# The row maxima of causal attention: mask addition and maximum in one VectorE instruction per score block

## The chip, the cores and the metric

The kernel runs on one core of one Trainium2 chip. The metric is the device time of one launch in microseconds (us); lower is better. The kernel before takes 1011.64 us, the median of three runs (1011.25 to 1013.38). The engines are named as in the profile: PE is TensorE's matrix multiplication and PEld its weight load, DVE is VectorE, ACT is ScalarE, POOL is GpSimd, SP is SyncE, whose queue (SPq) issues most transfers.

## The reference, cut to what matters

One layer of a decoder with four token mixers in parallel, on 1024 tokens (and 16 learned tokens ahead of them) of 1024 channels. The mixer that matters here is the attention with 8 heads; queries and keys have 96 channels, values 64:

```python
s = jnp.einsum('bqhd,bkhd->bhqk', qb, k).astype(jnp.float32)
q_pos = i * Q_BLOCK + jnp.arange(Q_BLOCK)
s = jnp.where(k_pos[None, :] <= q_pos[:, None], s, -jnp.inf)
p = jax.nn.softmax(s, axis=-1).astype(v.dtype)
return jnp.einsum('bqhk,bkhd->bqhd', p, v)
```

The other three mixers (pooling, a convolution module, a short gated convolution) and the gates come from the same input projection `h @ w_in`. At the end

```python
m = (gts[:, :, 0] * y_a + gts[:, :, 1] * y_b + gts[:, :, 2] * y_c + gts[:, :, 3] * y_d)
h_res = h_res + rms_norm(m @ w_o[i], post_norm_g[i])
```

## The kernel before, in words

Matrix products are made of float32 numbers split into a high and a low part (`split`, on ScalarE and mostly GpSimd), three matmuls for each product. The program has three stages, each recorded whole and then put in order:

- Stage 1, to about 658 us of the profile: the input projection, and in its gaps the work of the mixers that comes ahead of attention. Results go to DRAM: `q_dram`, `k_dram`, `kr_dram`, `v_dram`, the gates `th_dram`, the branch inputs `bo_dram`.
- Stage 2, to about 878 us: attention (`ps_s`, `ps_o`), with the output projections of the three other branches (`ps_y`) as work that fills TensorE's gaps.
- Stage 3: the output projection of the attention branch (`ps_u`), the product with `w_o`, and the norm.

**Attention, stage 2.** The work goes in 16 units: 8 heads h, and in each two halves c of 512 queries. Ahead of a unit's `attend(h, c)` stands its `maxima(h, c)` (from L1297), which finds the largest score of every query row, so that the exponentials stay in range. It takes four groups r of 128 queries. The scores of a group over its `nk = 16 + 128 * (4c + r + 1)` keys are computed roughly (one matmul on the high parts) in `nb` blocks of at most 512 columns, each in a PSUM bank `s`. For c = 0 the groups have 144, 272, 400 and 2 x 264 columns, for c = 1 2 x 328, 2 x 392, 2 x 456 and 348, 348, 344. To the last 128 columns of a group's last block VectorE adds the causal mask `maskS` (0 or -1e30), in PSUM; then it takes the maximum of each block into `mx[:, r, b]`. GpSimd fills `mx` with -1e30 ahead of this, for groups with fewer than three blocks. After the four groups one more maximum over `mx` gives `mr`, TensorE transposes `mr`, and VectorE writes the negated maxima into four extra rows of the query tile `qt` (its rows 96 to 99, against rows of ones in the key tile `kt`), so that the score matmuls of `attend` subtract the maximum themselves.

`attend` (from L1330) goes over blocks of 128 keys: three score matmuls into a bank `s`, a mask addition with `maskT` on the diagonal, the exponential `p` on ScalarE, its split into `pt` (high part on ScalarE, low part on GpSimd), and three matmuls with the values `vt` into `ps_o`.

There are five banks `s` for the maxima, the scores and the transposed `mr`, one bank `o`, and two banks `y` for the branch work. The key tile `kt` exists twice, so the keys of head h + 1 are loaded during head h: `load_kv` (L1285) issues them on SP's queue: keys, for the first two heads also the rotary keys `kt<-kr` that all heads share, then values. `load_q` (L1275) loads the queries of a unit.

**The branch work** comes from `fills` (L1408): 48 steps of 6 matmuls (288 in all), each step needing a weight tile `whl` (256 KB, five buffers) and a gate tile `th` (512 KB, three buffers) from DRAM, and ending on VectorE in a product with the gate (`m<-th,ps_y`, later `th<-th,ps_y` and an addition to `m`). `refill` (L1446) hands them out over the 16 units. The maxima run ahead of `attend` by a lead that `lead_to` (L1462) sets.

**The order** is not the order of recording. `Plan.record` (L293) gives every operation a cost (`cost`, L272: on VectorE 142 ns + 1.07 ns a column for most), its dependencies and a priority, and `flush` (L332) runs a list scheduler over each stage: whenever an engine is free, the operation with the lowest priority number that is ready and whose buffers are free comes next. The order that comes out is written into the engines' queues, and there each queue is worked through in order. So a change of costs or of operations changes the order on every engine in the rest of the stage. SBUF places come from the sizes of the tiles, pool by pool.

Of the kernel before, what the change touches and what calls it, by code (L numbers as in the profile page):

```python
# [21 lines left out]
F32 = mybir.dt.float32  # L22
# [3 lines left out]
ALU = mybir.AluOpType  # L26
AX = mybir.AxisListType
# [3 lines left out]
P = 128  # L31
# [11 lines left out]
NEG = -1e30  # L43
# [150 lines left out]
class Plan:  # L194
# [98 lines left out]
    def record(self, eng, op, args, kw):  # L293
        outs = [kw["out"] if "out" in kw else args[0]]
        ins = [v for v in list(args[0 if "out" in kw else 1:]) + [v for k, v in kw.items() if k not in ("out", "accum_out")]
               if hasattr(v, "shape")]
        cost, nbytes = self.cost(eng, op, outs, ins, kw.get("op") == ALU.pow)
        if kw.get("accum_out") is not None:
            outs.append(kw["accum_out"])
            cost += 190  # L300

        turns = eng == "POOL" and op != "dma_start" or eng == "DVE" and op != "tensor_reduce" and not any(
            isinstance(v, View) and v.buf.psum for v in outs + ins)
        o = {"i": len(self.ops), "turns": turns, "prio": len(self.ops) - self.lift, "eng": eng, "op": op, "args": args, "kw": kw,
             "cost": cost, "bytes": nbytes, "extra": 0 if getattr(getattr(outs[0], "buf", None), "dram", True) else self.extra, "bufs": set(), "deps": set() if self.wait is None else {self.wait}, "users": [], "end": None}
        for v, write in [(v, False) for v in ins] + [(v, True) for v in outs]:
            if not isinstance(v, View):
                continue
            b = v.buf
            if not write and not b.writes:  # L310
                raise RuntimeError(f"read before it is written: {op} {b.group['order'][0] is b} {v.shape}")
            for j, box in b.writes + (b.reads if write else []):
                if j != o["i"] and all(x[0] < y[1] and y[0] < x[1] for x, y in zip(box, v.box)):
                    o["deps"].add(j)
            if write:
                def rest(lst):
                    return [(j, box) for j, box in lst
                            if not all(y[0] <= x[0] and x[1] <= y[1] for x, y in zip(box, v.box))]
                b.writes, b.reads = rest(b.writes), rest(b.reads)
            (b.writes if write else b.reads).append((o["i"], v.box))  # L320
            o["bufs"].add(b)
        for b in o["bufs"]:
            b.left += 1
        self.ops.append(o)
        self.todo.append(o)
# [110 lines left out]
def trunk_kernel(ctx, tc, a):  # L436
    nc = tc.nc
    plan = Plan(nc)
    PE, ACT, DVE, POOL, SP = (plan.engine(e) for e in ("PE", "ACT", "DVE", "POOL", "SP"))
    ctx.enter_context(tc.manual_schedule())  # L440

    def pool(stack, **kw):
        return plan.open(stack, Pool(plan, stack.enter_context(tc.tile_pool(bufs=1, **kw)),
                                     psum=kw.get("space") == PSUM,
                                     side="dram" if kw.get("space") == DRAM else kw.get("side", "left")))
# [10 lines left out]
    def add(eng, out, x, y):  # L456
        eng.tensor_tensor(out, x, y, op=ALU.add)
# [57 lines left out]
    def bank(tag="x"):  # L515

        return psum.tile([P, 512], F32, tag=tag, bufs=2 if tag == "x" else 1, name=f"ps_{tag}")
# [731 lines left out]
    qk = pool(two, name="qk", reuse_waits="tile")  # L1249
    fp = pool(two, name="fp", reuse_waits="tile")  # L1250
    at = pool(two, name="at", reuse_waits="tile")
    cp = pool(ctx, name="cp", side="right", reuse_waits="tile")
    for d in range(4):
# [2 lines left out]
    boM = [[cp.tile([P, 2, 512], F32R, name=f"boM{i}{c}") for i in range(4)] for c in range(2)]  # L1256
    m_ = [[mpair[c][d // 2][:, d % 2] for d in range(KD)] for c in range(2)]

    maskS = qk.tile([P, P], F32, name="maskS")
    POOL.memset(maskS, 0.0)  # L1260
    POOL.affine_select(out=maskS, in_=maskS, compare_op=ALU.is_ge, fill=NEG,
                       base=0, pattern=[[-1, P]], channel_multiplier=1)
    maskT = qk.tile([P, P], F32, name="maskT")
    POOL.memset(maskT, 0.0)
    POOL.affine_select(out=maskT, in_=maskT, compare_op=ALU.is_ge, fill=NEG,
                       base=0, pattern=[[1, P]], channel_multiplier=-1)
# [4 lines left out]
                       base=0, pattern=[[-1, 4], [0, P]], channel_multiplier=1)  # L1271
# [25 lines left out]
    def maxima(h, c):  # L1297

        q_, k_ = qt[h, c], kt[h % 2]
        mx = at.tile([P, 4, 3], F32, tag="mx", bufs=2, name="mx")
        POOL.memset(mx, NEG)
        for r in range(4):
            nk = NM + P * (4 * c + r + 1)
            nb = -(-nk // 512)
            w_ = -(-nk // nb)
            w_ += w_ % 2
            n0 = 0  # L1310
            for b in range(nb):
                n = min(w_, nk - n0)
                s = bank("s")
                PE.matmul(s[:, :n], q_[:QK, 0, P * r:P * (r + 1)], k_[:QK, 0, n0:n0 + n], start=True, stop=True)
                if b == nb - 1:
                    add(DVE, s[:, n - P:n], s[:, n - P:n], maskS)
                DVE.tensor_reduce(mx[:, r, b:b + 1], s[:, :n], axis=AX.X, op=ALU.max)
                n0 += n
            yield
        mr = at.tile([P, 4], F32, tag="mr", bufs=2, name="mr")  # L1320
        DVE.tensor_reduce(mr, mx, axis=AX.X, op=ALU.max)
        pm = bank("s")
        PE.transpose(pm[:4, :P], mr, ident)
        DVE.tensor_tensor(q_[QK:NA, 0, :].rearrange("p (r n) -> p r n", n=P),
                          pm[:4, :P].unsqueeze(1).to_broadcast([4, 4, P]), negd, op=ALU.mult)
        yield
# [60 lines left out]
    op, smg = {}, {}  # L1387
# [69 lines left out]
    def ahead_of(i):  # L1457

        yield from maxima(*seq[i])
        lead["i"] = i + 1  # L1460
# [115 lines left out]
    for d in (0, 4, 1, 5, 2, 6, 3, 7):  # L1576
# [3 lines left out]
        for c in range(2):  # L1580
            t = th[:, 512 * c:512 * (c + 1)]
            py = bank("u")
            for k in range(4):
                b = boM[c][k]
# [142 lines left out]
```

## Time and profile before

| what | value |
|---|---|
| median of three runs | 1011.64 us (1011.25 to 1013.38) |
| profiled execution, span from first to last instruction (the page has no other time for it) | 1010.7 us |
| busy: PE, PEld, DVE, ACT, POOL | 988.6, 831.5, 683.4, 444.6, 680.8 us |
| mean granted TensorE clock | 0.993 |
| HBM read and written | 128.4 MB, 73.7 MB |

Two parts of the page give the course of the three stages: each digit is one fortieth of the span (25.3 us); busy shares are in tenths, and PEclk is the granted TensorE clock in tenths of full speed.

```profile
PE   9999999999999999999999999999999999999996
DVE  6846794897789679645435444265777777898547
POOL 6768766577575696777668645334569796647946
PEclk9999999999999999999999999998999999999998
```

In groups of instructions the columns are: line, engine, operation, output<-inputs with their shapes, the count; then the busy time in all and the mean ns of one; then the idle time of the engine just in front of them and what ended it. All recorded operations have the one line L330, where `issue` calls the engine, so the tiles' names tell them apart. In lists of waits: the waiting engine and tile, what it waited for, us in total, times, and the longest. In timelines: start, length, engine, operation and count, and in brackets the idle time in front. In windows: the stretch, its length, the busy time (and count) of PE, PEld, DVE, ACT and POOL, the granted TensorE clock, the busy share of the DMA engines, and GB/s.

### The profile page before, as it was taken

How to read it: one execution, taken by the hardware profiler on the slowest of the kernel's cores; microseconds unless marked ns; L12 is line 12 of the kernel's file. 1: busy time of each engine (PE TensorE's matmuls, PEld its weight loads, DVE VectorE, ACT ScalarE, POOL GpSimd, SP SyncE). 2: the span in 40 equal slices, each digit the busy share in tenths (PEclk: the TensorE clock that was granted, in tenths of full speed). 3: DMA queues.
4: the chain of work that ended last, by engine and by line, in shares of the span. 5: the costliest groups of instructions: out<-in, count | busy, mean ns of one | idle time of the engine just before them, and what ended most of it. 6: DMA issues, size and time to landing. Idle time of an engine off the chain costs nothing.

```text
span 1010.7 us, 15256 instructions
## 1 busy us (share of the span) xinstructions
PE 988.6 (98%) x5129; PEld 831.5 (82%) x5129; DVE 683.4 (68%) x1106; ACT 444.6 (44%) x895; POOL 680.8 (67%) x634
## 2 busy tenths in 40 slices
PE   9999999999999999999999999999999999999996
PEld 9999898889888877878778778867888788788885
DVE  6846794897789679645435444265777777898547
ACT  7633233443434455435444434225565656224632
POOL 6768766577575696777668645334569796647946
PEclk9999999999999999999999999998999999999998
DMA  7269656568676866955654643795857672673634
GB/s 247 75 211 308 231 162 194 185 206 287 204 263 214 293 185 206 299 181 159 205 178 158 190 143 115 229 348 174 242 158 245 185 230 75 247 251 99 192 98 166
DMA packets 126302, 203.13 MB, mean 201 GB/s; under 512 B 19650, under 2 KB 79161, under 8 KB 124880
## 3 DMA queue, kind: packets, MB, share of 16 engines
q1 hardware_dynamic: 121600, 185.38, 58.0%
q10 hardware_dynamic: 4336, 15.73, 4.2%
q8 instruction: 40, 0.66, 0.3%
q0 software_dynamic: 288, 1.05, 0.3%
q14 instruction: 38, 0.31, 0.1%
HBM read 128.40 MB, written 73.72 MB: 200 GB/s over the span
## 4 chain that ended last, share of the span: by engine, by line
PE 83%; DMA 5%; POOL 4%; DVE 4%; issue 3%; ACT 0%; SPq 0%; DVEq 0%; POOLq 0%; ACTq 0%
PE ps_pb L330 15%; PE ps_pa L330 14%; PE ps_pc L330 13%; PE ps_o L330 10%; PE ps_u L330 7%; PE ps_s L330 7%; PE ps_pd L330 6%; PE ps_y L330 6%; PE ps_x L330 4%; PE ps_w L330 1%; DMA vt<-v 1%; DMA th<-th 1%; POOL S L330 1%; DMA kt<-kr 1%; DVE op L330 1%
## 5 line engine op out<-in xcount | busy, mean ns | idle before, releaser
L330 PE MATMUL ps_pb<-T,S 128*128 128x512 f32 (+2 forms) x792 | 174.2, 363 | 0.1
L330 PE MATMUL ps_pa<-B,A 128*128 128x512 f32 (+2 forms) x792 | 172.0, 361 | 0.0
L330 POOL TENSOR_TENSOR S<-ss,S 128x512 fp32r<-128x512 f32 x84 | 114.2, 1370 | 73.4 <-ACT S L330 72.4
L330 PEld LDWEIGHTS ps_pa<-B,A 128*128 128x128 f32 x792 | 134.7, 188 | 23.9
L330 PEld LDWEIGHTS ps_pb<-T,S 128*128 128x128 f32 x792 | 133.7, 188 | 24.8 <-issue 1.7
L330 POOL TENSOR_TENSOR A<-raw,A 128x512 fp32r<-128x512 f32 x84 | 115.0, 1378 | 42.7 <-ACT A L330 42.5
L330 POOL TENSOR_TENSOR pt<-p,pt 128x512 fp32r<-128x512 f32 (+4 forms) x112 | 102.6, 942 | 48.7 <-PE ps_s L330 28.6
L330 DVE SCALAR_TENSOR_TENSOR ps_w<-conv,par,ps_w 128x512 f32<-128x512 f32 x116 | 87.3, 752 | 2.6
L330 PE MATMUL ps_pc<-T,S 128*128 128x512 f32 (+2 forms) x396 | 87.8, 363 | 0.5 <-DVE z L330 0.5
L330 PE MATMUL ps_pd<-T,A 128*128 128x512 f32 (+2 forms) x396 | 86.0, 362 | 0.0
L330 PE MATMUL ps_pc<-B,S 128*128 128x512 f32 (+2 forms) x396 | 85.8, 362 | 0.0
L330 PE MATMUL ps_y<-bo,whl 128*128 128x512 f32 x288 | 83.1, 407 | 0.6 <-DVE m L330 0.4
L330 ACT ACTIVATE p<-ps_s 128x512 f32<-128x512 f32 (+4 forms) x112 | 49.7, 444 | 73.8 <-PE ps_s L330 29.0
L330 ACT ACTIVATE S<-ss 128x512 fp32r<-128x512 f32 x84 | 51.0, 628 | 69.7 <-DVE ss L330 39.9
L330 PEld LDWEIGHTS ps_pc<-B,S 128*128 128x128 f32 x396 | 67.3, 188 | 12.3 <-issue 0.5
L330 PEld LDWEIGHTS ps_pd<-T,A 128*128 128x128 f32 x396 | 67.2, 188 | 11.9
L330 PEld LDWEIGHTS ps_pc<-T,S 128*128 128x128 f32 x396 | 66.7, 188 | 12.4 <-DVE z L330 0.7
L330 PE MATMUL ps_o<-pt,vt 128*128 128x512 f32 (+4 forms) x336 | 73.8, 335 | 1.8 <-ACT ol L330 1.6
L330 PE MATMUL ps_s<-qt,kt 100*128 100x512 f32 (+4 forms) x336 | 68.5, 330 | 0.7 <-DVE qt L330 0.7
L330 ACT ACTIVATE A<-raw 128x512 fp32r<-128x512 f32 x84 | 52.3, 625 | 35.6 <-PE ps_pd L330 19.3
L330 PEld LDWEIGHTS ps_o<-pt,vt 128*128 128x128 f32 x336 | 52.7, 175 | 15.1 <-ACT ol L330 3.2
L330 PEld LDWEIGHTS ps_s<-qt,kt 100*128 100x128 f32 x336 | 56.1, 183 | 10.7 <-issue 0.9
(341 smaller groups left out, 1895.1 us busy)
## 6 DMA issues: line engine op xcount, KB each, us to landing
raw<-in_w_in_dram SPq DMA_DIRECT2D x56, 512.0 KB
th<-th SPq DMA_DIRECT2D x32, 512.0 KB
th<-z ACTq DMA_DIRECT2D x30, 512.0 KB
v<-vhl SPq DMA_DIRECT2D x16, 384.0 KB
qt<-q SPq DMA_DIRECT2D x16, 384.0 KB
bo<-bo SPq DMA_DIRECT2D x6, 1024.0 KB
vt<-v SPq DMA_DIRECT2D x8, 768.0 KB
kt<-k SPq DMA_DIRECT2D x8, 520.0 KB
```

Source lines behind the costliest of these rows:

```text
L330: getattr(self.handle[o["eng"]], o["op"])(*map(real, o["args"]), **{k: real(v) for k, v in o["kw"].items()})
```

## The change

In `maxima` the mask addition, the maximum of a block and the last maximum over `mx` are replaced. Where a group has only one block, or the block is not its first, one instruction `tensor_tensor_reduce` adds a mask to the block (the sum is written back to PSUM) and takes the maximum of the sum and a start value: -1e30, or for a block that is not the first the maximum of the block ahead of it, read per partition from `mx`. The maximum of the last block of a group goes straight into `mr[:, r]`. The first block of a group with several blocks keeps its plain maximum. `mx` is two columns wide and no longer filled ahead. `maskS` becomes 512 columns wide: its last 128 are the causal mask and the others 0, so that its last n columns are the mask of a last block with n columns, and its first n columns are zeros, for the middle block of the group with three blocks. In the planner the extra 190 ns for an instruction with a second output stay for ScalarE alone.

```diff
         if kw.get("accum_out") is not None:
             outs.append(kw["accum_out"])
-            cost += 190
+            cost += 190 if eng == "ACT" else 0
...
-    maskS = qk.tile([P, P], F32, name="maskS")
+    maskS = qk.tile([P, 512], F32, name="maskS")
     POOL.memset(maskS, 0.0)
     POOL.affine_select(out=maskS, in_=maskS, compare_op=ALU.is_ge, fill=NEG,
-                       base=0, pattern=[[-1, P]], channel_multiplier=1)
+                       base=512 - P, pattern=[[-1, 512]], channel_multiplier=1)
...
-        mx = at.tile([P, 4, 3], F32, tag="mx", bufs=2, name="mx")
-        POOL.memset(mx, NEG)
+        mx = at.tile([P, 4, 2], F32, tag="mx", bufs=2, name="mx")
+        mr = at.tile([P, 4], F32, tag="mr", bufs=2, name="mr")
...
-                if b == nb - 1:
-                    add(DVE, s[:, n - P:n], s[:, n - P:n], maskS)
-                DVE.tensor_reduce(mx[:, r, b:b + 1], s[:, :n], axis=AX.X, op=ALU.max)
+                last = b == nb - 1
+                if b == 0 and not last:
+                    DVE.tensor_reduce(mx[:, r, :1], s[:, :n], axis=AX.X, op=ALU.max)
+                else:
+                    mask = maskS[:, 512 - n:] if last else maskS[:, :n]
+                    DVE.tensor_tensor_reduce(out=s[:, :n], in0=s[:, :n], in1=mask, scale=1.0,
+                                             scalar=mx[:, r, b - 1:b] if b else NEG, op0=ALU.add, op1=ALU.max,
+                                             accum_out=mr[:, r:r + 1] if last else mx[:, r, b:b + 1])
                 n0 += n
             yield
-        mr = at.tile([P, 4], F32, tag="mr", bufs=2, name="mr")
-        DVE.tensor_reduce(mr, mx, axis=AX.X, op=ALU.max)
```

## The prediction

> **What bounds the kernel now.** I read the page from its busy shares to its chain, then the attention stage by stretches, then the waits of TensorE there.
>
> ```profile
> span 1010.7 us, 15256 instructions
> PE 988.6 (98%) x5129; PEld 831.5 (82%) x5129; DVE 683.4 (68%) x1106; ACT 444.6 (44%) x895; POOL 680.8 (67%) x634
> PE 83%; DMA 5%; POOL 4%; DVE 4%; issue 3%; ACT 0%; SPq 0%; DVEq 0%; POOLq 0%; ACTq 0%
> ```
>
> TensorE (PE) is busy for 98% of the span and is 83% of the chain that ends last; VectorE (DVE), where the change is made, has 4% of the chain. So VectorE time is worth only what TensorE loses by waiting for it. The maxima pass lies between about 658 and 850 us. The next view is TensorE's waits from 655 to 860, then windows (busy of PE, PEld, DVE, ACT, POOL; granted TensorE clock; DMA share; GB/s).
>
> ```profile
> PE ps_s L330 <- DMA kt<-kr: 3.7, 1, 3.7
> PE ps_o L330 <- ACT ol L330: 1.6, 3, 1.2
> PE ps_s L330 <- DVE qt L330: 0.7, 1, 0.7
> PE ps_y L330 <- DVE m L330: 0.4, 1, 0.4
> ...
> 652.00:675.00 23.00, 22.64 (x101) 17.99 (x99) 10.08 (x23) 2.87 (x4) 5.51 (x13) 1.00 1.03 408
> 675.00:684.60 9.60, 5.15 (x25) 3.76 (x24) 6.99 (x19) 3.78 (x10) 3.74 (x6) 0.89 1.01 228
> 684.60:689.40 4.80, 4.80 (x19) 4.44 (x20) 1.38 (x4) 0.60 (x1) 0.00 (x0) 0.50 0.40 110
> 700.00:860.00 160.00, 158.41 (x857) 133.02 (x856) 121.93 (x293) 93.76 (x210) 120.01 (x134) 1.00 0.65 194
> ```
>
> Two things are to be seen. From 700 to 860 TensorE idles only 1.6 us of 160, with VectorE busy for 122 (76%): there is next to nothing to win there. The stage's loss is at its opening: TensorE waits 3.7 us for the second head's keys (`kt<-kr`), and then 4.8 us of work run at half clock (0.50), which costs 4.8 x 0.5 = 2.4 us more. These 6.1 us are the largest loss of the stage, and what moves them decides the change.
>
> **The change, part by part.** VectorE first:
>
> ```profile
> L330 DVE TENSOR_TENSOR ps_s<-ps_s,maskS 128x128 f32<-128x128 f32 x64 | 18.1, 291 | 4.6 <-PE ps_s L330 4.2
> L330 DVE TENSOR_REDUCE mx<-ps_s 128x1 f32<-128x144 f32 (+6 forms) x112 | 55.2, 507 | 8.0 <-PE ps_s L330 5.4
> L330 DVE TENSOR_REDUCE mr<-mx x16: 166/166/167, 673.8 to 848.0; 128x4 f32<-128x12 f32 x16
> L330 DVE TENSOR_REDUCE mx<-ps_s 128x1 f32<-128x456 f32 x16 | 10.1, 629 | 0.9 <-PE ps_s L330 0.6
> L330 DVE TENSOR_TENSOR z<-ps_pc,u 128x512 f32<-128x512 f32 x46 | 31.7, 690 | 19.8 <-PE ps_pc L330 19.0
> L330 DVE SCALAR_TENSOR_TENSOR ps_w<-conv,par,ps_w 128x512 f32<-128x512 f32 x116 | 87.3, 752 | 2.6
> L330 DVE TENSOR_TENSOR ss<-raw,ss 128x512 f32<-128x512 f32 x28 | 36.8, 1313 | 6.9 <-POOL S L330 6.9
> ```
>
> Removed: 64 mask additions (18.1 us) and 16 last maxima (16 x 0.166 = 2.7 us), 20.8 us together. Of 112 block maxima 40 stay; 72 become the combined instruction (9 blocks a head: the last block of each of 8 query groups, and the middle one of the only group with three blocks). No row shows that instruction, so its price is bounded. Going by a two-operand instruction on the same kind of operands (one in PSUM, one in SBUF), the rows at 128 and 512 columns (291 and 690 ns) give 1.04 ns a column and 158 ns; at 456 columns that is 632 ns against 629 for the maximum it replaces: no difference. 48 of the 72 read a start value per partition, which the `ps_w` row prices at 752 - 690 = 62 ns: 3.0 us. The built kernel's instruction order shows a second small instruction behind each of the 72, the write of the maximum; nearest row 166 ns, so 0 to 12.0 us, and I take 12.0, since no row of a VectorE instruction is shorter than about that. VectorE then loses 20.8 - 3.0 - 12.0 = 5.8 us of work, at best 20.8. The other bound is the `ss` row, 1313 ns where both operands are in SBUF: (1313 - 690) / 512 = 1.22 ns more per column, over the 72 blocks' 23584 columns 28.7 us more, so 23 us added. I take the near rows: the mask addition already has the same operands in the same places.
>
> The Trainium skill (VectorE: DVE Perf Modes, "Two Vector instructions with no wait between them") says that an operation that also writes out its accumulator is two instructions, the main one and an accumulator read; this speaks against "one instruction per block". The built order agrees; by it the saving is 5.8 us, without it 17.8 us.
>
> What hides this VectorE time is TensorE's own work: the 1.6 us of idling in 700 to 860 is all that less VectorE work can return. I set the term to 0, with -1.6 to +1.5: the planner prices the second instruction at nothing, so VectorE runs behind its plan by up to 72 x 0.166 us in small pieces, and TensorE meets a late PSUM bank now and then. If that cover were gone, the 5.8 us would be the price. GpSimd loses 16 memsets and their waits:
>
> ```profile
> L330 POOL MEMSET mx<- 128x12 f32 x16 | 1.6, 106 | 13.9 <-DVE mr L330 12.8 <-PE ps_o L330 1.0
> L330 POOL MEMSET maskS<- 128x128 f32 x1 | 0.2, 224 | 0.0
> L330 POOL TENSOR_SCALAR_AFFINE_SELECT negd<-negd 4x512 f32<-4x512 f32 x1 | 0.6, 633 | 0.1
> L330 POOL MEMSET negd<- 4x512 f32 x1 | 0.5, 517 | 0.0
> ```
>
> Of the 13.9 us in front of them, 8.5 lie before any attention work is queued on GpSimd, so I count 0. The mask of 512 columns costs 0.5 + 0.6 us by the `negd` rows, 0.6 more than now, at 661 us; it is first needed behind three merge steps on VectorE near 664. 0.
>
> **What the planner moves** matters more. The order of all engines is made by a planner from its costs, and the changed costs reorder TensorE from the third attention matmul to the stage's end. In the built order the second head's first key matmul, the one that waits above, has 30 branch matmuls (`ps_y`) of this stage in front of it, not 60; the first unit's 15 score matmuls and its first 4 value matmuls, now in front, come behind it. On SP's queue the second head's loads stand behind 3 `th` and 4 `whl` loads where there are now 7 and 8 (counted from the second `bo` load). Rows:
>
> ```profile
> 660.06 7.89 PE L330 MATMUL ps_y<-bo,whl 128*128 128x512 f32 x33
> ...
> 675.80 1.89 PE L330 MATMUL ps_s<-qt,kt 100*128 100x512 f32 x9 [0.65 <-DVE qt L330]
> ...
> 679.84 0.92 PE L330 MATMUL ps_o<-pt,vt 128*128 128x512 f32 x3
> 680.60 0.32 PE L330 MATMUL ps_s<-kt,qt 96*128 96x344 f32 x1
> 684.59 0.78 PE L330 MATMUL ps_s<-kt,qt 96*128 96x144 f32 x2 [3.67 <-DMA kt<-kr]
> 672.48 0.42 SPq L330 DMA_DIRECT2D qt<-q  x1
> 673.47 1.04 SPq L330 DMA_DIRECT2D kt<-kr  x2
> whl<-w_out_pool SPq DMA_DIRECT2D x8, 256.0 KB
> th<-th SPq DMA_DIRECT2D x7, 512.0 KB
> ```
>
> TensorE's side: 30 x 7.89/33 = 7.2 us of branch work, about 2.0 us for the 15 (nine take 1.89 with the weights' waits in them; the last six have few columns) and 1.0 for the four: 10.2 us less in front, so TensorE gets there at 680.9 - 10.2 = 670.7, or some us earlier where waits of now vanish. The loads' side: 4 x 256 KB + 4 x 512 KB = 3.1 MB less in front, at the 408 GB/s of the saturated stretch 7.7 us. If the rest takes as long as now, the keys land at 684.6 - 7.7 = 676.9. If query and keys (384 + 520 + 2 x 130 KB, 1.2 MB) were moved at 408 GB/s and not at the 228 of the 9.6 us from 675, they would land at 675.0 - 7.7 + 2.9 = 670.2. I take 675.0, nearer to the upper end, since the same loads follow one another in the same order. Either way the keys decide, not the branch work: at the landing TensorE has done 10.2 us less than now at 684.6, so the opening gets better by 684.6 - 10.2 - T = 674.4 - T, with T the landing: -0.6 us at 675.0, that is 0.6 us slower; bounds -4.2 (faster) and +2.5 (slower). The stall is then 4 to 5 us in place of 3.7, the half-clock stretch behind it stays.
>
> On that stretch the Trainium skill (TensorE: Matmul & The Clock Gate, "HAM oscillation — how this bites in real kernels") has the rule that idle gaps up to about 3.4 us keep the clock. The stall here began at 680.9 and the clock was down before 683:
>
> ```profile
> 682.00:683.00 1.00, 0.00 (x0) 0.00 (x0) 0.12 (x1) 0.00 (x0) 0.25 (x2) 0.79 0.90 240
> 683.00:684.00 1.00, 0.00 (x0) 0.00 (x0) 0.00 (x0) 0.00 (x0) 0.00 (x0) 0.50 0.92 292
> ```
>
> By the row a stall of 2 us already costs the 2.4 us; by the rule it would not. At my 4 to 5 us both say cold.
>
> **Sum.** The profiled span is 1010.7; the median 1011.64 lies 0.9 above it, which I take for what lies around the span. 1010.7 + 0.9 + 0.6 (opening) + 0 (VectorE) + 0 (GpSimd) = 1012.2 us.
>
> **Rivals.** (a) *The keys come early*: T near 670 to 671, where TensorE arrives. The stall shrinks to under 2 us and with it the half clock: 4.2 + up to 2.4 us faster, 1005.0 to 1007.5, say 1006.5. For it: the DMA queues have nothing else to wait for. Against: the same loads crawl at 228 GB/s now. (b) *VectorE's relief comes through*: TensorE's 1.6 us in mid-stage and the 1.1 us of `qt` and `m` waits go, 1009.3 with T as forecast. Against: these waits are for latencies, not for a busy VectorE. (c) *The opening has too little cover* (slower): keys at 676.9 (+2.5), and since the first unit's scores now run behind the stall, their exponential, split and GpSimd half stand open on the path. By rows below that is 0.60 + 0.63 + 1.3 = 2.5 us, less what TensorE still has to do then; 1.0 to 1.5 us left: 1010.7 + 0.9 + 2.5 + 1.2 = 1015.3. It decides from T above about 676. For it: 30 branch matmuls fewer early, which is what filled such gaps. Against: the cold score matmuls themselves take longer than that chain.
>
> ```profile
> 677.11 0.60 ACT L330 ACTIVATE p<-ps_s 128x512 f32<-128x512 f32 x1 [16.76 <-DVE ps_s L330]
> 677.79 0.63 ACT L330 ACTIVATE pt<-p 128x512 fp32r<-128x512 f32 x1
> L330 POOL TENSOR_TENSOR pt<-p,pt 128x512 fp32r<-128x512 f32 x47 | 61.0, 1321 | 44.8 <-PE ps_s L330 28.0 <-ACT pt L330 13.6 <-issue 3.2
> ```
>
> (d) *The combined instruction runs at the `ss` row's rate*: VectorE gets 23 us more in about 190, from 76% to 88% busy; TensorE then waits for PSUM banks, by my estimate a quarter of it, 5.8 us: 1018. Against: 291 ns with a PSUM operand. (e) *It does not do what it says*: with its second instruction a block costs what mask and maximum cost, VectorE's work stays, and the opening alone decides: the forecast's time.
>
> **Chances.** Forecast 0.38, (a) 0.16, (b) 0.09, (c) 0.25, (d) 0.08, (e) 0.04. A change under 0.2% (2.0 us) can't be told from none here, so "same" is 1009.6 to 1013.7. The forecast and (e) lie mostly within, (a) and (b) count as faster, (c) and (d) as slower: faster 0.27, same 0.38, slower 0.35. The forecast's own range is 1010 to 1014.5; to hold 8 in 10 it must take in most of (a) and (c): 1007 to 1016.5.
>
> **What would show it.** TensorE's waits: one wait on `kt<-kr` between 668 and 677, longer than 3.7 us, and a stretch of 0.50 clock behind it (under 2 us and no 0.50: (a)). Windows of 700 to 860 shifted: TensorE idling 1 to 3 us, VectorE nearer 70%. The groups: 72 combined instructions at 310 to 700 ns, and 72 small ones at or under 170 ns; near 1 us at 456 columns it is (d). The forecast is wrong if the opening's loss changes by over 3 us, or if TensorE's idling after 700 exceeds 4 us.

## The result: 0.49% slower, all of it in the attention stage

| | before | after |
|---|---|---|
| median | 1011.64 us (5 runs, 1011.11 to 1013.38) | 1017.20 us (5 runs, 1015.88 to 1019.35) |
| ratio, 95% interval | | 1.0049 [1.0036, 1.0062] |
| profiled execution: span | 1010.7 us | 1015.4 us |
| first maxima matmul of stage 2 | 658.70 us | 658.71 us |
| first `ps_u` matmul (stage 3) | 877.96 us | 882.64 us |

The change costs about 5 us (5.6 by the medians, 4.7 by the two profiled spans). The forecast was 1012.2 with a range of 1007 to 1016.5, so the time lies outside. The stages before and behind the attention stage are alike; stage 2 is 223.93 us long where it was 219.26, 4.67 us more, the whole difference of the spans.

The page of the changed kernel (span, busy time by engine, the chain that ended last):

```profile
span 1015.4 us, 15278 instructions
PE 988.9 (97%) x5129; PEld 832.7 (82%) x5129; DVE 674.4 (66%) x1098; ACT 444.3 (44%) x895; POOL 679.2 (67%) x618
PE 86%; DMA 3%; DVE 3%; issue 3%; POOL 3%; ACT 1%; SPq 0%; DVEq 0%; ACTq 0%; POOLq 0%
```

VectorE did get 9.0 us less to do (683.4 before). The time is not there: TensorE idles more. Its waits in stage 2 of the changed kernel, from 655 to 885 us:

```profile
PE ps_s L330 <- DMA kt<-kr: 6.8, 1, 6.8
PE ps_o L330 <- ACT ol L330: 2.4, 1, 2.4
PE ps_y L330 <- DVE lcp L330: 1.0, 1, 1.0
```

The wait for the second head's keys has grown from 3.7 to 6.8 us, and one wait of 2.4 us for a copy of the value bank is new. Windows of the changed kernel (busy of PE, PEld, DVE, ACT, POOL; granted clock; DMA share; GB/s), the last one the whole stage:

```profile
652.00:669.70 17.70, 16.93 (x75) 13.12 (x73) 8.51 (x22) 2.87 (x4) 5.87 (x10) 1.00 1.04 392
669.70:676.54 6.84, 0.04 (x2) 0.03 (x1) 2.65 (x8) 0.00 (x0) 0.00 (x0) 0.70 0.98 230
676.54:686.00 9.46, 9.45 (x29) 7.74 (x30) 4.61 (x14) 4.17 (x11) 3.67 (x5) 0.50 0.55 185
700.00:820.00 120.00, 120.00 (x651) 101.53 (x649) 79.85 (x217) 69.15 (x155) 87.34 (x90) 1.00 0.73 223
820.00:840.00 20.00, 17.58 (x94) 14.31 (x93) 16.22 (x32) 10.93 (x27) 16.93 (x17) 1.00 0.45 141
658.71:882.64 223.93, 212.46 (x1105) 176.20 (x1104) 152.38 (x368) 111.14 (x248) 148.41 (x151) 0.97 0.67 211
```

And of the kernel before, for the same parts:

```profile
700.00:820.00 120.00, 118.58 (x642) 99.58 (x641) 89.84 (x221) 69.11 (x154) 90.24 (x101) 1.00 0.73 216
820.00:840.00 20.00, 20.00 (x111) 16.95 (x110) 17.07 (x40) 13.29 (x32) 18.44 (x21) 1.00 0.56 180
658.70:877.96 219.26, 212.21 (x1105) 175.10 (x1104) 160.45 (x375) 110.95 (x247) 146.89 (x166) 0.98 0.68 212
```

The last rows give the balance. TensorE's idle time in the stage is 223.93 - 212.46 = 11.47 us, 7.05 before: 4.42 more, of which the keys' wait is 6.80 - 3.67 = 3.13. In the opening the half clock also holds for 9.46 us of work in place of 4.80. In 700 to 820 TensorE now idles not at all (1.42 us before), which is all that VectorE's relief returns, and in 820 to 840 it loses 2.42 us that it did not lose.

### The profile page after: what moved, and what is told of

Its sections match the earlier page's. It is cut to its first block, busy times and chain, and to the rows that moved or that the text cites. A ratio compares the mean times of both kernels' runs of the same rounds, so it can differ in the third digit from the quotient of the medians.

```text
span 1015.4 us, 15278 instructions
## 1 busy us (share of the span) xinstructions
PE 988.9 (97%) x5129; PEld 832.7 (82%) x5129; DVE 674.4 (66%) x1098; ACT 444.3 (44%) x895; POOL 679.2 (67%) x618
## 4 chain that ended last, share of the span: by engine, by line
PE 86%; DMA 3%; DVE 3%; issue 3%; POOL 3%; ACT 1%; SPq 0%; DVEq 0%; ACTq 0%; POOLq 0%
PE ps_pb L330 15%; PE ps_pa L330 14%; PE ps_pc L330 13%; PE ps_o L330 10%; PE ps_s L330 8%; PE ps_u L330 7%; PE ps_pd L330 7%; PE ps_y L330 6%; PE ps_x L330 4%; DMA kt<-kr 1%; POOL S L330 1%; PE ps_w L330 1%; DMA whl<-w_out_pool 1%; DVE ps_w L330 1%; DMA th<-th 1%
## 5 line engine op out<-in xcount | busy, mean ns | idle before, releaser
L330 PE MATMUL ps_y<-bo,whl 128*128 128x512 f32 x288 | 85.4, 404 | 0.5 <-DMA whl<-w_out_pool 0.2
L330 PE MATMUL ps_s<-qt,kt 100*128 100x512 f32 (+4 forms) x336 | 72.1, 341 | 0.0
```

The costliest lines, as they stand in the source:

```text
L330: getattr(self.handle[o["eng"]], o["op"])(*map(real, o["args"]), **{k: real(v) for k, v in o["kw"].items()})
```

## The experiments

**Theory 1**: the reordered opening costs the time; the keys come earlier, but TensorE has too little work in front of them. **Theory 2**: the combined instruction itself costs it, in any order. Letters are added where a rival came up later. All times stand against runs of the kernel before on the same chip, with a median of 1012.17, 1011.77 and 1011.67 us in the three groups (e1 to e4, e5 to e8, e9 to e11); the ratio has its 95% interval.

**e1: the order of after, the instructions of before.** The order is planned with the combined instruction, and each one is replaced where it is issued:

```diff
+        if k["last"]:
+            tail = real(k["out"][:, n - P:])
+            v.tensor_tensor(tail, tail, real(k["in1"][:, n - P:]), op=ALU.add)
+        v.tensor_reduce(top, s, axis=AX.X, op=ALU.max)
+        if isinstance(start, View):
+            v.tensor_tensor(top, top, real(start), op=ALU.max)
```

> Order of all engines as in the changed kernel, instructions on VectorE as before: each combined instruction is issued as the mask addition on the last 128 columns, the plain maximum, and, where there is a start value, a maximum of two columns of one element. Theory 1 (the reordered opening of the attention stage costs the time, the instruction does not): as slow as the changed kernel, 1016 to 1019 us, with one wait of 6 to 7 us for the second head's keys and about 13 us at half clock. Theory 2 (the combined instruction itself costs the time, in any order): near the kernel before, 1011 to 1013 us. Both halves: in between, near 1014.5.

Measured: 1034.92 us, 1.0217 [1.0196, 1.0238]. Nobody expected this. TensorE's waits in stage 2, and the stage as one window:

```profile
PE ps_s L330 <- DVE mr L445: 5.4, 8, 1.4
PE ps_s L330 <- DMA kt<-kr: 3.7, 1, 3.7
PE ps_s L330 <- DVE mx L330: 3.2, 4, 1.9
```

```profile
658.60:900.51 241.91, 224.87 (x1105) 180.95 (x1104) 181.25 (x408) 111.00 (x248) 148.76 (x151) 0.94 0.63 194
```

VectorE has 181.25 - 152.38 = 28.9 us more work than in the changed kernel. TensorE waits for the maxima (`mr`, `mx`), which the order expects sooner, in short stalls all through the stage, idles 17.04 us and runs at a mean clock of 0.94. Both theories miss the size. The experiment is not a pure undoing, since 48 blocks now take two or three old instructions where the kernel before had one or two, and these additional ones, maxima of two columns of one element, are 27.3 of the 28.9 us:

```profile
L445 DVE TENSOR_TENSOR mr<-mr,mx 128x1 f32<-128x1 f32 x40 | 23.0, 575 | 1.4
L445 DVE TENSOR_TENSOR mx<-mx 128x1 f32<-128x1 f32 x8 | 4.3, 534 | 0.3
```

The 40 of the first row take 168 ns in the median and up to 3787 ns; the last section comes back to the long ones. So e1 prices mainly an instruction that neither kernel has. It shows that in this order 28.9 us more on VectorE are not hidden, and it says little about the combined instruction; that question rests on e2.

**e2: the order of before, the combined instruction.** In effect (the edit marks the operations and exchanges them when they are issued):

```diff
-    add(DVE, s[:, n - P:n], s[:, n - P:n], maskS)
-    DVE.tensor_reduce(mx[:, r, b:b + 1], s[:, :n], axis=AX.X, op=ALU.max)
+    DVE.tensor_tensor_reduce(out=s[:, :n], in0=s[:, :n], in1=wide[:, 512 - n:], ...)
```

(for the last block of a group, when it is issued; the planner still counts the old pair).

> Order of all engines as in the kernel before, instructions on VectorE as in the changed kernel: the mask additions are left out, the last block's maximum of each query group is the combined instruction with the wide mask and, where there is one, a start value; the last small maximum of a head and its memset stay. Theory 1 (the opening's order costs the time): as the kernel before or a little faster, 1009.5 to 1012 us. Theory 2 (the instruction costs it): slower than before by 3 to 5 us, 1014.5 to 1017, with more waits of TensorE for score banks between 700 and 860 us.

Measured: 1012.28 us, 0.9998 [0.9984, 1.0012]. The stage as one window:

```profile
658.61:878.63 220.02, 213.28 (x1106) 175.65 (x1104) 148.98 (x375) 110.80 (x247) 147.43 (x167) 0.98 0.68 211
```

VectorE has 11.5 us less work than before (148.98 against 160.45) and the time is the same. Theory 2, with its 1014.5 to 1017, falls; and as far as an unchanged order goes, the 11.5 us of VectorE's time are worth nothing that the interval (about 1.4 us either way) could show.

**e3: after, with TensorE kept at work during the wait.**

```diff
+            for _ in range(28):
+                self.handle["PE"].matmul(out, q_, k_, start=True, stop=True)
```

> The changed kernel with 28 additional matmuls (96x128 by 96x512, their result is overwritten by the next matmul) in front of the second head's first key matmul, so that TensorE is at work during most of its wait for the keys. They cannot bring the keys earlier. If half of the loss is the longer half-clock stretch behind the stall (4.7 us lost there against 2.4 before): the stretch behind the stall goes and the time is 1012 to 1013.5 us. If the loss is the stall and the order alone and the clock only follows: 1016.5 to 1018, or more if the additional matmuls themselves run at half clock.

Measured: 1015.61 us, 1.0022 [1.0009, 1.0036]: 1.6 us below the changed kernel by the medians (0.27% by the ratios, which is 2.7 us), less than expected. In the profiled execution stage 2 began 1.6 us later (660.30) and was 3.1 us shorter (220.82 us); whether it begins late in the others isn't known. From the second head's first key matmul to the third transposition of `mr`, the same 78 matmuls, first in e3 (row 1 is the 28 additional ones):

```profile
672.35:678.82 6.47, 6.47 (x28) 5.36 (x29) 2.42 (x7) 0.00 (x0) 0.00 (x0) 1.00 0.98 255
678.82:693.18 14.36, 14.27 (x78) 11.55 (x77) 6.46 (x21) 11.79 (x26) 10.45 (x11) 1.00 0.32 104
```

and in the changed kernel:

```profile
676.54:694.71 18.17, 18.16 (x78) 14.96 (x79) 6.68 (x21) 11.87 (x26) 10.57 (x11) 0.74 0.29 97
```

18.17 - 14.36 = 3.8 us is what the half clock costs there, and the lead is still 3.8 us at the first `ps_u` matmul (206.10 against 202.30 us behind the keys). Half of the 9.46 us would have been 4.7. Behind the stage's start the keys' first matmul came 0.7 us later than in the changed kernel, which is why the stage gains 3.1 and not 3.8.

**e4: after, with more work planned in front of the keys.** The planner is told that the second head's loads land later; its order then keeps 24 score and 15 value matmuls ahead of them.

```diff
-                load_kv(h + 1)
+                with plan.slow(9000 if h == 0 else 0):
+                    load_kv(h + 1)
```

> The changed kernel, whose planner is told that the second head's loads land 9 us later than it thinks; loads are issued as in the changed kernel, but TensorE now has 24 score matmuls and 15 value matmuls of the first unit and 36 branch matmuls in front of the second head's first key matmul (0, 0 and 30 in the changed kernel). Theory 1 (too little work is left in front of that wait): the wait of 6.8 us shrinks below 2 us, the half clock with it, 1009 to 1012.5 us. Theory 2 (the instruction costs it): 1016 to 1018. If the keys land later when more is moved in front, or the work merely changes places: 1014 to 1016.

Measured: 1010.19 us, 0.9977 [0.9963, 0.9990]. The 7.0 us between this and the changed kernel come from where matmuls stand, with the same instructions. The wait for the keys is gone. From about 705 us in the changed kernel and 699 us here, the two timelines of TensorE have nearly the same order to the stage's end, so the hint acts on the opening. The two openings, up to the same matmul (changed kernel, then e4):

```profile
658.71:705.14 46.43, 38.84 (x188) 32.03 (x187) 24.85 (x72) 17.75 (x42) 21.19 (x28) 0.85 0.71 223
659.40:699.00 39.60, 38.35 (x191) 31.66 (x190) 25.57 (x75) 17.88 (x41) 21.22 (x28) 0.91 0.87 271
```

The opening is 46.43 - 39.60 = 6.8 us shorter. The execution profiled (1013.94 us) is the slowest of twelve; in it the clock fell to half twice, at 671.7 us for 6.8 us although TensorE was at work, and at 828.7 us for 3.4 us (last section), and the wait of 2.4 us for a copy of the value bank is still there.

**e5: before, with the same hint** (6000 in place of 9000, which puts 23 score and 15 value matmuls in front of the keys).

> The kernel before (old instructions), whose planner is told that the second head's loads land 6 us later: 68 branch, 23 score and 15 value matmuls in front of the second head's first key matmul (60, 15 and 4 in the kernel before); the loads' order is that of before. Theory 1 (the time hangs on how much work covers that wait, in either kernel): its wait of 3.7 us and the half clock behind it go or halve, 1007 to 1011 us, as fast as the changed kernel with the same hint or faster. Rival 1b (the order found with the old prices has no use for more cover, the gain of the changed kernel with the hint came from the cheaper maxima): no faster than before, 1011.5 to 1014.

Measured: 1011.19 us, 0.9991 [0.9978, 1.0004]. The keys' wait is gone here too, in the profile (of the fastest of the twelve executions), but the medians show no gain that can be told from none. New waits for `mx` (2.4 us) stand in the list in its place: the covered order waits for VectorE's old maxima.

**e6: after, with the planner's line undone.** All instructions are those of the changed kernel; only the planner again counts 190 ns for the second instruction behind each combined one.

```diff
-            cost += 190 if eng == "ACT" else 0
+            cost += 190
```

> The changed kernel with the planner's line undone: the planner again counts 190 ns for the second instruction behind each combined one. In front of the second head's first key matmul stand 30 branch, 15 score and 1 value matmuls (30, 0, 0 in the changed kernel); the loads as in the changed kernel. Theory 1 (cover in front of that wait): 15 score matmuls more in front give about 2.4 us at full clock, so a wait of 4 to 5 us instead of 6.8 and a half-clock stretch that is still there: 1013 to 1016.5 us. Rival 1c (the planner's price of the second instruction matters for the whole stage, since VectorE is late against its plan 72 times): 1010 to 1012.5. If it changes nothing: 1016 to 1018.5.

Measured: 1010.91 us, 0.9985 [0.9972, 0.9997]: 6.3 us below the changed kernel, so rival 1c's number. TensorE in the opening:

```profile
671.46 0.42 PE L330 MATMUL ps_s<-kt,qt 96*128 96x344 f32 x1 [0.30 <-DVE mr L330]
672.03 2.76 PE L330 MATMUL ps_s<-qt,kt 100*128 100x512 f32 x15 [0.15 <-DVE mx L330]
674.76 0.50 PE L330 MATMUL ps_o<-pt,vt 128*128 128x512 f32 x1
675.75 0.31 PE L330 MATMUL ps_s<-kt,qt 96*128 96x144 f32 x1 [0.49 <-ACT pt L330]
```

The 15 score matmuls stand in front of the keys again, and the key matmul at 675.75 waits for something else and not for the keys. This execution, the fastest of twelve, got there later by itself (1.3 us of waiting for a weight tile up to 664.16), so that little work sufficed. The line moves more than this, however: TensorE's order differs from the changed kernel's through the whole stage, and the wait for the value bank's copy is 1.1 us here and not 2.4. Whether 1c works through the opening or through the whole stage is asked by e8.

**e7: the hint of e4, and a late contention taken away.** The new wait of 2.4 us, in the changed kernel's timeline:

```profile
826.21 7.06 DVE L330 TENSOR_TENSOR op<-ol,rb 64x512 f32<-64x512 f32 x2
...
828.36 3.76 POOL L330 TENSOR_TENSOR pt<-p,pt 128x512 fp32r<-128x512 f32 x3
833.30 0.60 ACT L330 ACTIVATE ol<-ps_o 128x512 f32<-128x512 f32 x1 [3.07 <-DVE op L330]
...
833.95 0.73 PE L330 MATMUL ps_o<-pt,vt 128*128 128x512 f32 x2 [2.42 <-ACT ol L330]
```

Two multiplications on VectorE, with a median of 679 ns each over the kernel, take 7.06 us here, the first of them 6457 ns; GpSimd works without a pause from 824.43 until the last of these `pt` ends at 832.12. ScalarE's copy waits for them, and TensorE for the copy.

```diff
-        mul(DVE, op[c][64 * e:64 * (e + 1), :], ol[h][:64, c], rb)
+        mul(POOL if h == 4 else DVE, op[c][64 * e:64 * (e + 1), :], ol[h][:64, c], rb)
```

> The changed kernel with the hint of 9 us, and the two multiplications of the fifth head's output by its reciprocal sums (64x512, both operands in SBUF) on GpSimd instead of VectorE, where the second of them took 6.5 us beside GpSimd's own work and TensorE then waited 2.4 us for the copy of the value bank. If that wait is late because VectorE and GpSimd hold each other up: the wait of 2.4 us goes, 2 to 3.5 us faster than with the hint alone, 1007 to 1008.5. If GpSimd's 2.6 us more delay the next exponentials' halves instead: 1009.5 to 1012.

Measured: 1006.59 us, 0.9944 [0.9925, 0.9963]: 3.6 us below e4, faster than both kernels. The waits that are left in stage 2, and the stage:

```profile
PE ps_s L330 <- DVE mr L330: 1.0, 3, 0.5
PE ps_y L330 <- DVE th L330: 1.0, 2, 0.6
```

```profile
658.87:871.31 212.44, 208.89 (x1106) 173.24 (x1104) 145.81 (x366) 111.33 (x248) 148.20 (x153) 1.00 0.71 220
```

TensorE idles 3.55 us in the stage and has the full clock; neither the keys nor `ol` are in the list. In e4's profile half clock followed that wait, in the changed kernel's it did not, so a part of the 3.6 us may be the clock.

**e8: the hint of e4 and the planner's line undone.**

> The changed kernel with the hint of 9 us and with the planner's line undone: 32 branch, 19 score and 15 value matmuls in front of the second head's first key matmul. If the price of the second instruction matters behind the opening (rival 1c): faster than the hint alone, 1006.5 to 1009. If the cover alone matters (theory 1): the same as the hint alone within its run-to-run spread, 1009 to 1012.

Measured: 1009.86 us, 0.9971 [0.9958, 0.9985], against 0.9977 for the hint alone. Where the opening is covered, the planner's line makes no difference in the sum, which speaks for its acting mainly through the opening. It is not a clean separation: in e8 the longest wait for `ol` is 1.1 us and the longest of the 14 multiplications 1950 ns, so the late contention is small here, and yet e8 is not faster than e4 by what e7 won. Either something else in its order costs that again, or e7's gain is not the wait's alone; this was not traced.

**e9: after, with e7's second edit alone.**

> The changed kernel, with only the two multiplications of the fifth head's output on GpSimd; the opening is that of the changed kernel (30 branch matmuls in front of the second head's first key matmul). This prices the late wait of 2.4 us by itself. If the opening costs the most and the late wait its 2.4 us: 1013.5 to 1015.5 us, with the wait of 6.8 us and its half clock still there. If the gain of 3.6 us that the same edit brought behind the covered opening holds here too: 1013 to 1014. If TensorE's lost time is only found again further on: 1016 to 1018.

Measured: 1015.24 us, 1.0030 [1.0019, 1.0042], about 2 us below the changed kernel. In this profile the keys' wait was 5.2 us, and the lead on the changed kernel was 0.6 us at the transposition in front of the removed wait (823.07 against 823.68), 3.6 at the next (832.56 against 836.14) and 2.2 at the first `ps_u` matmul. Half of the 3 us won is lost again.

**e10: before, with the hint and e7's second edit.**

> The kernel before (old instructions) with the hint of 6 us and the same two multiplications on GpSimd. It shows what the combined instruction is worth where the opening is covered: the changed kernel with both edits took 1006.6 us. If the combined instruction is worth nothing there: 1006 to 1008. If VectorE's relief is worth 1 to 3 us once the opening is covered: 1008.5 to 1011.

Measured: 1008.88 us, 0.9973 [0.9961, 0.9986], against 0.9944 for the same two edits with the combined instruction. So the combined instruction is worth about 2 to 3 us once the opening is covered, as far as two orders that a planner made, with hints of 6 and 9 us, differ in nothing else.

**e11: all three** (line undone, hint, second edit).

> The changed kernel with the planner's line undone, the hint of 9 us and the two multiplications on GpSimd: a candidate for the best. If the two gains add (line undone or hint, and the late wait): 1005 to 1008 us. If, with the planner's line undone, VectorE's and GpSimd's late meeting was small already (two multiplications of 2.55 us together, not 7.06): as without the edit, 1008.5 to 1011.

Measured: 1011.21 us, 0.9995 [0.9984, 1.0006]. The gains don't add; with the line undone the two multiplications took only 2.55 us together in e8, so there was little to win, and in this profile the clock was at half from 671.7 to 678.5 us. Why it fell there is open.

## Why the prediction was wrong, by its steps

**What bounds the kernel: right.** TensorE's waits at the opening decided, not VectorE's 76%.

**VectorE's term, 0 with -1.6 to +1.5: right on the order of before** (e2). The groups of the changed kernel (the first mixes six widths, the second is the widest alone), and a piece of VectorE's timeline:

```profile
L330 DVE CUSTOM_DVE_ANT_0 ps_s<-ps_s,maskS,mx 128x264 f32<-128x264 f32 (+5 forms) x48 | 28.4, 594 | 11.9 <-PE ps_s L330 7.0 <-ACT pt L330 0.2
L330 DVE CUSTOM_DVE_ANT_0 ps_s<-ps_s,maskS,mx 128x456 f32<-128x456 f32 x8 | 5.6, 701 | 1.2 <-PE ps_s L330 0.2
L330 DVE DVE_READ_ACCUMULATOR2_ANT mr<- 128x1 f32 x64 | 8.9, 139 | 0.1
```

```profile
665.32 0.14 DVE L330 DVE_READ_ACCUMULATOR2_ANT mr<- 128x1 f32 x1
665.32 0.48 DVE L330 CUSTOM_DVE_ANT_0 ps_s<-ps_s,maskS 128x272 f32<-128x272 f32 x1
```

At 456 columns with a start value the prediction's rows give 158 + 1.04 x 456 + 62 = 694 ns, and it took 701. The second instruction takes 139 ns, not 166 (the kernel before has rows of 131 to 159 ns for one to four columns, which the forecast overlooked), and in the timeline it starts at the same moment as the next instruction, so little of it counts: VectorE lost 9.0 us of work over the span where 5.8 were forecast. The small rows bear out what the Trainium skill has (VectorE: DVE Perf Modes, "Two Vector instructions with no wait between them"), that the accumulator's write is an instruction of its own; that it runs beside the next one is this trace's. Rival (d), the rate of the `ss` row, is out. The sum of rival (b) is 1009.5 by its own terms (1012.2 - 1.6 - 1.1), not 1009.3; nothing hung on it.

**The opening: the step that failed.** The prediction had "the opening gets better by 674.4 - T", with T = 675.0, and "the half-clock stretch behind it stays", together 0.6 us of loss.
- T was 676.5, close to the upper bound (676.9), where the forecast took 675.0. While TensorE waited the queues moved 230 GB/s, as slowly as before: the bound in which "the rest takes as long as now" was the better estimate. The DMA engines' busy share was 0.98 in that window, and 1.01 beside the 228 GB/s in the prediction's own: they were not waiting for work, so no row spoke for 408 GB/s at this place. Why these transfers move slowly was not traced.
- By the formula T alone is 2.1 us of loss; the wait grew by 3.1. The other 1.0 is the work in front: TensorE was there at 669.74 (forecast 670.7), 11.2 us earlier than before and not 10.2.
- The half clock did not stay as it was. It held for 9.46 us of work and cost 3.8 us (e3), in place of 4.80 us of work before. Half of these is the 2.4 us of the prediction; at the rate of e3 (3.8 / 9.46) it is an estimated 1.9, and e5, the old instructions at full clock, has 212.21 - 210.34 = 1.9 us less TensorE work in the stage than the kernel before. So the clock costs about 1.9 us more, an estimate from orders that are not the same.

Together some 5 us, against the 0.6. Rival (c), too little cover, 1015.3 us, had the right mechanism, its condition (T above about 676) and most of the size (2.5 + 1.2 us); it had 0.25. Its second part, the open chain of the exponential, is not what came: the additional loss was the clock. The forecast's own condition for failing, an opening worse by over 3 us, is met.

**The planner's line.** The prediction charged it only with VectorE being late against its plan in small pieces, at most 1.5 us. It is the line that moved the 15 score matmuls behind the keys: e6 has every instruction of the changed kernel, without that line, and is 6.3 us faster. That the opening is worth this much is shown by e4, whose order behind it is nearly the changed kernel's. How much of e6's own 6.3 us is the opening is not shown: its order is another one throughout, and by e9 some 1.5 to 2 us of it can be the late wait.

**Not foreseen**: the 2.4 us at 834 us, of which e9 finds some 1.5 us at the stage's end and 2 us in the medians. TensorE's idling after 700 (160 - 157.58 = 2.4 us up to 860) stayed below the 4 us that would have spoken against the forecast; the relief of 1.42 us by 820 lies within its -1.6. The balance of the stage: 3.1 (keys) + 2.4 (value bank) - 1.4 (relief) and 0.3 elsewhere are the 4.42 us of idling, and TensorE's busy time grew by 0.25, where the clock alone makes about 1.9 more. The other 1.7 us are work that the new order needs less: without a half clock TensorE is busy for 210.34 us of the stage with the old instructions (e5), and for 215.12 - 6.47 = 208.65 in e3 without its 28 additional matmuls. Why, was not traced.

**Around the span** lie 1.7 to 2.1 us in the executions where both times are known (e2: 1013.08 and 1011.4; e9: 1015.3 and 1013.2), not 0.9; nothing hung on it.

## What to carry to other kernels

Where a scheduler makes the order, the edit of its price list is a part of the change with a cost of its own: run the changed instructions with the old prices too. Work that stands in front of a load is worth what it hides, and if the load comes some us earlier with less work in front of it, the stall can still grow, and with it the time at half clock. When a bound depends on how fast the last transfers move, the rate shown at that very place beats the rate of a better stretch, above all where the DMA engines are already busy at the low rate.

## What the runs showed of the hardware that was not expected

The clock comes back after very different times. In the changed kernel it fell and rose in these windows:

```profile
672.00:673.00 1.00, 0.00 (x0) 0.70 0.97 145
...
686.00:687.00 1.00, 1.00 (x7) 0.97 0.04 16
```

(busy of PE alone, clock, DMA share, GB/s). A window's clock is the mean of 1 and 0.50, which gives the moment of the change: at half clock from 672.4 to 686.06 it is 13.66 us, 9.5 of them with TensorE at work without a gap; before, by the prediction's rows and the one at 689 us (0.80), it is 682.58 to 689.40, 6.82 us, 4.8 of them at work. One is twice the other, and e1's, read in the same way (673.38 to 683.62, 10.24 us), three halves of the shorter. In e4 the clock fell behind short pauses alone:

```profile
671.72:678.54 6.82, 6.82 (x23) 5.84 (x23) 4.68 (x14) 3.55 (x9) 3.24 (x4) 0.50 0.98 283
```

the waits just ahead were of 0.29 to 0.33 us each, and e7 had the same waits in its profile and kept the clock. Later in the same execution it fell again, behind the wait of 2.42 us for the value bank:

```profile
828.00:829.00 1.00, 0.47 (x2) 0.87 0.26 96
829.00:832.00 3.00, 3.00 (x11) 0.50 0.00 0
832.00:833.00 1.00, 1.00 (x8) 0.93 0.00 0
```

That is 3.4 us of half clock, from 828.74 to 832.14, half of the 6.82; the changed kernel had the same wait of 2.42 us and kept the clock. So the lengths 3.4, 6.82, 10.24 and 13.66 are one, two, three and four times about 3.41 us; a gap's length alone does not say whether the clock falls, nor dense work how soon it returns. The twelve runs of e4 lie between 1007.43 and 1013.94 us; that this stretch makes the spread was not tried.

A VectorE instruction can wait long beside GpSimd. The 14 multiplications of 64x512 in stage 2 of the changed kernel (shortest, median, longest in ns):

```profile
L330 DVE TENSOR_TENSOR op<-ol,rb x14: 674/679/6457, 737.1 to 877.7; 64x512 f32<-64x512 f32 x14
```

The longest covers five GpSimd instructions in a row (826.21 to 832.12). The Trainium skill (SBUF — State Buffer, "Who interferes with whom") says that a VectorE instruction with two inputs in SBUF and a GpSimd instruction that reads SBUF block each other, and that the later one waits for the earlier. The trace agrees that it waits, but it waited for a whole row of them and not for one; with the two on GpSimd (e7) they took 1.28 us each and the wait was gone. e1's small maxima, again with two inputs in SBUF, show it too. The longest, and GpSimd beside it:

```profile
767.71 4.91 POOL L330 TENSOR_TENSOR pt<-p,pt 128x512 fp32r<-128x512 f32 x6
770.08 3.79 DVE L445 TENSOR_TENSOR mr<-mr,mx 128x1 f32<-128x1 f32 x1
772.58 1.26 POOL L330 TENSOR_TENSOR m<-m,th 128x512 f32<-128x512 f32 x1
```

It ends at 773.87, just behind the last of GpSimd's row at 773.84. 168 ns in the median became 3787 ns for one column, so the size of such an instruction does not say what it costs beside a busy GpSimd.
